# A two-block network on one core: narrow gate products, mLSTM decay rows, the first norm and the compressed values rewritten

## The chip, the cores and the metric

The kernel runs on one core of a Trainium2 chip, as one launch. The metric is the device time of one execution in microseconds; lower is better. All data are float32 in DRAM; the kernel's products have to agree with a float32 reference.

## The reference

512 latent tokens and 256 context tokens of width 1024 go through two hybrid layers; after these the latent tokens alone go through a second block. Cut to what the change touches:

```python
def hybrid_layer(l, x, xc, sc, scc, ...):                 # l = 0, 1
    h = rms_norm(x, norm_g) * (1 + scale[:, None]) + shift[:, None]     # 512 tokens
    hc = rms_norm(xc, norm_g) * (1 + scale_c) + shift_c                 # 256 tokens
    aq, ak, av, az, bq, bk, bv, bo, bz, bg, cq, ... = split_proj(h @ w_in)
    # branch a: differential attention; branch b: mLSTM in both directions, gates from bg (16 columns)
    # branch c: neighbourhood attention; then the three are merged

def mlstm_chunkwise(q, k, v, log_i, log_f, state, with_out):
    ...
    dmat = jnp.where(causal, b[..., :, None] - b[..., None, :] + li[..., None, :], -jnp.inf)
    m_t = jnp.maximum(b + m[..., None], jnp.max(dmat, axis=-1))
    qk = jnp.einsum('bthd,bshd->bhts', qc, kc) * jnp.exp(dmat - m_t[..., None])
    num = a_inter[..., None] * (q @ C) + jnp.einsum('bhts,bshv->bhtv', qk, vc)
    ...

def second block(x):        # hybrid (LRU and retention), ffn, nsa, ffn
    # nsa: 16 heads of width 64 in 4 groups; each head adds three attentions, weighted by
    # sigmoid gates (48 columns of the projection): over compressed keys and values,
    # over selected blocks, and over a window
```

## The kernel before

Activations lie feature-major: eight chunks of 128 features by 768 (or 512) tokens. TensorE takes float32 products in two ways. The large projections split both operands into a high and a low part of a faster format (`slot` casts the raw weights on ScalarE into `whi` and subtracts on VectorE into `wlo`; `make_h` gives `hh` and `hl`) and add three products, hi by hi, hi by lo and lo by hi. `proj` issues these three per chunk, all at line 345; a token-major projection does so at line 402 (`tm_step`). Small products take float32 operands as they are, which shows as two matmul instructions each.

A list scheduler orders each engine's instructions by a simulation of the program; only in `start`, the beginning of layer 0, is the order of PE, DVE and ACT the program's own. Raw weights come through the SP queue into a ring of three tiles, the parts stand in rings of four. PSUM tiles are named `pj` (large) and `s` (small).

The order of the work in one hybrid layer: norm and modulation (`start` in layer 0, `residual_0` in layer 1), branch a, a merge, the gates of branch b (`gates`), its four heads (`mlstm` in each), a merge, branch c, a merge. What the change touches:

- **`start`** (lines 611 to 680) loads the latent chunks `xs`, then the context chunks. ScalarE squares each chunk and VectorE adds it into `ssq` (`sumsq`, line 539), once over the latents and then over the context. Four matmuls with a vector of ones (line 547) sum over the features, `rstd` raises to -1/2 on POOL (line 549), `rows` spreads the result over 128 partitions in PSUM (line 554), `R` is its SBUF copy. Products of a modulation vector (line 486) are turned through line 488 and line 746 into `mod` and the gain `G` (lines 494, 504, 508). A chunk is multiplied by `R` (lines 650, 657, 661, and for chunks 2 to 7 line 673, alternately on VectorE and POOL); then `make_h` makes `hh` on ScalarE (line 576: scale and shift), the same on VectorE in float32 (line 577), and `hl` (line 579). `silu_c`, the input of the modulation, comes first on ScalarE (line 463). Layer 1's `residual_0` multiplies by the row factors at line 1329 and calls the same `make_h`.
- **`gates`**: `proj` makes 16 rows of 768 tokens (24 matmuls of 512 columns and 24 of 256), then six transposes at line 990 turn them. **`nsa_gates`** does the same for 48 rows of 512 tokens (24 matmuls at line 345, four transposes at line 1819). The list scheduler places the latter beside `compress`, whose chain from the compressed keys ends in `kc` and the scores at line 1893.
- **`mlstm`**: for each chunk of 128 tokens and each direction, one transpose of a broadcast column of `Q` (line 1099) writes a matrix whose rows are all equal; VectorE adds the causal mask `MK` and puts the sum into `D` (line 1101), ScalarE takes the exponential, VectorE multiplies by the scores (line 1132), and TensorE takes it as an operand (line 1138). Each direction's `D` has one buffer, so that the next head's first write to it waits for the last use at line 1138. `Q` is ready once per layer (line 1054).
- **`nsa_values`**: per unit (one block of 128 queries of a pair of heads, 32 units), one product of the compressed values, with 64 of the 128 rows (line 1968, two instructions), and then products of the values with the turned weights at line 1972, 64 columns of the array each. It is a generator: `nsa_step` turns four blocks of the next unit's weights (line 746) and lets the generator take one step, by turns.

Of the kernel before, what the change touches and what calls it, by code (L numbers as in the profile page):

```python
# [13 lines left out]
P = 128  # L14
# [148 lines left out]
def make_plan():  # L163
# [5 lines left out]
    pl.tab("arope", 2 * SEQ, da_rope)  # L169

# [108 lines left out]
class Ker:  # L279
# [76 lines left out]

    def pj(self, cols=512, rows=P):
        return self.t(self.psum, [P, 512], F32, "pj", 2)[:rows, :cols]
# [59 lines left out]
    def run(self):  # L418
        tc, nc = self.tc, self.nc
        self.NRING = 4  # L420
        with self.pool("const", 1, "left") as cp, self.pool("ring", 2, "left") as ring, \
# [18 lines left out]
            self.contrib = dram.tile([2, KD, P, TT], F32, name="contrib")  # L440
            self.xsave = dram.tile([KD, P, SEQ], F32, name="xsave")
            self.mods = {}
            self.silu_c()
# [11 lines left out]
    def silu_c(self):  # L455
        nc = self.nc
        self.cl = self.t(self.cp, [P, KD, 32], F32, "cl")
        nc.vector.memset(self.cl, 0.0)
        with self.pool("sc", 1) as sp:
            c = self.t(sp, [P, KD, 2], F32, "c")  # L460
            th = self.t(sp, [P, KD, 2], F32, "th")
            nc.scalar.dma_start(c, self.ap["cv"].rearrange("p (k t) -> p k t", t=2))
            nc.scalar.activation(th, c, AF.Tanh, scale=0.5)
            nc.vector.tensor_scalar_mul(c, c, 0.5)
            nc.vector.scalar_tensor_tensor(self.cl[:, :, 0:2], th, 1.0, c, ALU.add, ALU.mult)

# [74 lines left out]
    def rstd(self, r, ssqs, n):  # L541

        nc = self.nc
        ps = self.s1()
        for i, ssq in enumerate(ssqs):
            for c in range(n):
                nc.tensor.matmul(ps[:, c:c + 1], ssq[:, P * c:P * c + P], self.ones[:, 0:1], start=i == 0, stop=i == len(ssqs) - 1)
# [15 lines left out]
    def make_h(self, l, xs, js, part=None):  # L563
# [4 lines left out]
        for j in js:  # L568
# [42 lines left out]
    def start(self):  # L611

        nc = self.nc
        with self.pool("x0", 8) as xp, self.pool("nt", 1) as sp:
# [9 lines left out]
            ssq = self.t(sp, [P, TT], F32, "ssq")  # L624
# [12 lines left out]
            def stats(c):  # L637
                n = (c.stop - c.start) // P
                r = self.t(sp, [P, 8], F32, "rstd", 2)[:, :n]
                self.rstd(r, [ssq[:, c]], n)  # L640
                return r

            E = mybir.EngineType
            with self.tc.manual_schedule(engines={E.PE, E.DVE, E.Activation}):
                squares(lat)
                rl = stats(lat)
                squares(ctx)
                fin = self.mod_products(units[0], self.s1)
                rows(lat, rl)
                nc.vector.tensor_mul(xs[0][:, lat], rs[:, lat], xs[0][:, lat])  # L650
                fin()
                rc = stats(ctx)
                self.make_h(0, xs, (0,), (lat,))
# [3 lines left out]
                nc.vector.tensor_mul(xs[1][:, lat], R[:, lat], xs[1][:, lat])  # L657
                fin()
                self.make_h(0, xs, (1,), (lat,))
                for j in range(2):  # L660
                    nc.vector.tensor_mul(xs[j][:, ctx], R[:, ctx], xs[j][:, ctx])
                    self.make_h(0, xs, (j,), (ctx,))
                ps = self.tm_banks(NTC, True)
                for s in range(4):
                    j = 2 * s + 2
                    parts = self.tm_step("av", 0, s, ps, 4 * (s == 0), slot)
                    if s < 3:
# [4 lines left out]
                        for i in range(2):  # L672
                            (nc.vector, nc.gpsimd)[i].tensor_mul(xs[j + i], R, xs[j + i])
# [3 lines left out]
                        self.make_h(0, xs, (j,))  # L677
                        next(parts)
                        fin()
                        self.make_h(0, xs, (j + 1,))  # L680
# [243 lines left out]
    def branch_b(self, l):  # L924
        tc, nc, T = self.tc, self.nc, self.T
        full = l == 0
        with self.pool("bb1", 1) as cp:
            with self.pool("bg", 1) as gp:
                G = self.gates(l, cp, gp)
            with self.pool("bb", 2) as sp:  # L930
# [8 lines left out]
                for h in range(4):  # L939
# [23 lines left out]
                    self.mlstm(T // P, h, qk["q"], qk["k"], V, G, hb, ss, sp)  # L963
# [11 lines left out]
    def gates(self, l, cp, sp):  # L975
# [5 lines left out]
        slot = self.slot(("bg", l))  # L981
# [1015 lines left out]
```

## Time and profile before

| | us |
|---|---|
| median of three runs | 3148.14 (3148.11 to 3149.46) |
| the profiled execution | 3147.98 |
| its span, first to last instruction | 3146.2 |
| PE (matmul) busy | 3078.2 |
| VectorE busy | 1797.7 |
| ScalarE busy | 1257.6 |
| POOL busy | 300.9 |

The profile is of one execution. Matmul ends overlap, so the time that one costs is read from start to next start, not from its own duration. In rows of the timeline the columns are start, duration, engine, line, operation, output and inputs, shapes, count, and in brackets the idle time ahead of it and what ended that.

### The profile page before, as it was taken

Reading aid. Unit: us, or ns where it says so; the run is one execution under the profiler, and the core shown is the slowest. Engines: PE = TensorE matmul, PEld = TensorE weight load, DVE = VectorE, ACT = ScalarE, POOL = GpSimd, SP = SyncE. Lnnn points to the kernel's source line nnn. Section 1 sums busy time; section 2 is a strip of 40 time slices with the busy share of each in tenths; the row PEclk is TensorE's granted clock in tenths of the full one; section 3 lists DMA queues with packets and bytes.
Section 4 is the critical chain, followed back from the end, with each engine's and each line's share of the span. In section 5 each row is a group of like instructions: output and inputs, shape, how many; then the busy total and the mean of one; then the engine's idle time right before and its main releaser. Section 6 shows DMA issues by size and latency. Waiting matters only on the chain.

```text
span 3146.2 us, 43890 instructions
## 1 busy us (share of the span) xinstructions
PE 3078.2 (98%) x17322; PEld 2572.0 (82%) x17322; DVE 1797.7 (57%) x3477; ACT 1257.6 (40%) x2382; POOL 300.9 (10%) x284
## 2 busy tenths in 40 slices
PE   7999999999999999999999999999999999999998
PEld 5888788888888888788888877788888788788887
DVE  6776256735574577346455477754433688644433
ACT  4553244325432356234344444332322267632221
POOL 1000000000015000000000400101100022101100
PEclk9999999999999999999999999999999999999999
DMA  6113211332235211311332533233223310022322
GB/s 225 41 34 135 71 60 48 127 115 72 84 138 205 87 49 48 111 54 61 110 104 88 161 100 102 67 101 101 94 94 104 99 41 28 28 94 94 101 92 69
DMA packets 86894, 285.96 MB, mean 91 GB/s; under 512 B 10400, under 2 KB 15264, under 8 KB 86304
## 3 DMA queue, kind: packets, MB, share of 16 engines
q1 hardware_dynamic: 68832, 237.60, 22.6%
q0 software_dynamic: 7424, 28.32, 2.5%
q10 hardware_dynamic: 10432, 17.24, 1.8%
q8 instruction: 136, 2.23, 0.3%
q14 instruction: 70, 0.57, 0.1%
HBM read 268.44 MB, written 14.68 MB: 90 GB/s over the span
## 4 chain that ended last, share of the span: by engine, by line
PE 88%; DVE 7%; issue 2%; ACT 2%; POOL 1%; DMA 0%; ACTq 0%; DVEq 0%; POOLq 0%
PE pj L345 57%; PE s L345 10%; PE s L746 4%; PE s L402 3%; PE s L741 2%; PE pj L402 2%; PE s L742 2%; PE s L1263 1%; PE pj L1972 1%; PE s L878 1%; PE s L1119 1%; DVE kl L737 1%; PE s L1145 1%; PE s L1138 1%; DVE kl L736 1%
## 5 line engine op out<-in xcount | busy, mean ns | idle before, releaser
L345 PE MATMUL pj<-hl,whi 128*128 128x512 f32 (+3 forms) x2696 | 939.5, 367 | 0.3 <-DVE hl L332 0.2
L345 PE MATMUL pj<-hh,whi 128*128 128x512 f32 (+3 forms) x2696 | 936.4, 369 | 2.6 <-ACT hh L331 0.8
L345 PE MATMUL pj<-hh,wlo 128*128 128x512 f32 (+3 forms) x2696 | 938.2, 367 | 0.0
L319 ACT CAST whi<-raw 128x1024 fp32r<-128x1024 f32 (+2 forms) x391 | 405.4, 1038 | 1088.8 <-PE pj L345 841.0
L320 DVE TENSOR_TENSOR wlo<-raw,whi 128x1024 fp32r<-128x1024 f32 (+2 forms) x391 | 488.1, 1249 | 443.4 <-ACT whi L319 434.4
L345 PEld LDWEIGHTS pj<-hh,whi 128*128 128x128 f32 (+2 forms) x2696 | 483.6, 187 | 92.7 <-issue 3.0
L345 PEld LDWEIGHTS pj<-hl,whi 128*128 128x128 f32 (+2 forms) x2696 | 483.0, 187 | 85.0 <-issue 1.9
L345 PEld LDWEIGHTS pj<-hh,wlo 128*128 128x128 f32 (+2 forms) x2696 | 482.9, 187 | 84.3 <-issue 1.7
L345 PE MATMUL pj<-uh,whi 128*128 128x512 f32 (+1 forms) x374 | 141.0, 377 | 0.0
L345 PE MATMUL pj<-ul,whi 128*128 128x512 f32 (+1 forms) x374 | 140.8, 376 | 0.0
L345 PE MATMUL pj<-uh,wlo 128*128 128x512 f32 (+1 forms) x374 | 140.8, 376 | 0.0
L741 PE MATMUL s<-kh,q 128*128 128x256 f32 (+1 forms) x320 | 101.2, 334 | 8.7 <-ACT kh L735 3.3
L700 ACT ACTIVATE th<-pj 128x512 f32<-128x512 f32 x72 | 37.3, 521 | 162.0 <-PE pj L345 150.3
L1715 DVE TENSOR_TENSOR a<-a,pj 128x512 f32<-128x512 f32 x44 | 30.3, 688 | 121.5 <-PE pj L345 121.5
L345 PE MATMUL s<-yh,whi 128*128 128x512 f32 (+1 forms) x288 | 98.7, 357 | 0.0
L345 PE MATMUL s<-yh,wlo 128*128 128x512 f32 (+1 forms) x288 | 98.0, 354 | 0.0
L345 PE MATMUL s<-yl,whi 128*128 128x512 f32 (+1 forms) x288 | 97.8, 354 | 0.0
L1713 POOL TENSOR_TENSOR a<-a,R 128x512 f32<-128x512 f32 x44 | 56.9, 1292 | 409.6 <-DVE a L1712 409.6
L1709 DVE TENSOR_TENSOR a<-pj,R 128x512 f32<-128x512 f32 x44 | 30.4, 691 | 113.5 <-PE pj L345 113.5
L742 PE MATMUL s<-kl,q 128*128 128x256 f32 (+1 forms) x320 | 92.7, 315 | 0.0
L345 PE MATMUL s<-hl,whi 128*128 128x512 f32 (+1 forms) x288 | 89.5, 347 | 0.0
L345 PE MATMUL s<-hh,wlo 128*128 128x512 f32 (+1 forms) x288 | 88.1, 345 | 0.0
(493 smaller groups left out, 4991.4 us busy)
## 6 DMA issues: line engine op xcount, KB each, us to landing
raw<-in_w SPq DMA_DIRECT2D x392, 512.0 KB, 3.4
mraw<-in_w SPq DMA_DIRECT2D x30, 512.0 KB, 4.9
bias<-in_bias ACTq DMA_DIRECT2D x16, 768.0 KB, 4.8
contrib<-cb POOLq DMA_DIRECT2D x16, 384.0 KB, 3.2
ld<-contrib POOLq DMA_DIRECT2D x16, 384.0 KB, 4.0
raw<-in_w SPq DMA_DIRECT2D x16, 384.0 KB, 2.9
contrib<-cb POOLq DMA_DIRECT2D x16, 256.0 KB, 2.6
ld<-contrib POOLq DMA_DIRECT2D x16, 256.0 KB, 3.1
```

What stands on the lines that cost most here:

```text
L319: nc.scalar.copy(hi[:, :width], raw[:, :width])
L320: nc.vector.tensor_sub(lo[:, :width], raw[:, :width], hi[:, :width].bitcast(F32))
L345: self.mm = self.nc.tensor.matmul(ps, wt[:, off + k * mcols:off + (k + 1) * mcols], acts[k][which][:, r], start=first and i == 0, stop=las ...
L402: self.nc.tensor.matmul(ps[c], self.h[k][a][:, P * c:P * c + P], b[:, w], start=k == 0 and pi == 0, stop=k == KD - 1 and pi == 2)
L700: self.nc.scalar.activation(th[:, r], p_, AF.Tanh, scale=0.5)
L736: nc.vector.tensor_sub(kl[a, c], r[a, c], kh[a, c].bitcast(F32))
L737: nc.vector.tensor_sub(kl[b, c], r[a, c], kh[a, c].bitcast(F32))
L741: self.nc.tensor.matmul(out, q[:, qs], kh[:, ks], start=True, stop=False)
L742: self.nc.tensor.matmul(out, q[:, qs], kl[:, ks], start=False, stop=True)
L746: self.nc.tensor.transpose(out[:, P * i:P * i + P], b, self.tab["id"])
L878: nc.tensor.matmul(po, at[:, P * i:P * i + P], V[:, k0 + i, P * h:P * h + P], start=i == 0, stop=i == nb - 1)
L1713: nc.gpsimd.tensor_mul(a, a, self.R)
```

## The change

- **Gates.** A new `narrow` writes the high part of the weights and the low part beside each other into one tile of 2n columns; for each chunk there are two matmuls instead of three, one by `hh` and one by `hl`. The result has 2n rows; the transposes that follow become float32 products by a stacked identity (`sum16`, `sum48`, loaded from the table), which adds the two halves. In `nsa_gates` the row factor is applied after that.
- **Decay rows.** `Q` is transposed once per layer (48 rows), stored into a DRAM tile, and for each head and direction loaded into `D` with every row sent to all 128 partitions. VectorE adds the mask in place.
- **First norm.** In `start` the squares of two chunks are added and then summed by TensorE into one PSUM tile over the four pairs; `silu_c` moves behind the latent squares and the context squares behind the cast of the first weight slot. `make_h` takes the unscaled chunk: one VectorE operation multiplies by `G` and `R`, ScalarE adds the shift only, and `hl` comes from one operation. The separate multiplications by `R` go away, also in layer 1.
- **Compressed values.** `VC` has two forms with zeros in the other half of the rows, so that the product takes all 128 rows. `nsa_values` is no longer a generator: it runs whole ahead of the transposes. A few small tiles move to another ring.

```diff
+    def narrow(self, key, n, outs):
+        raw = self.raw(key)[:, :KD * n].rearrange("p (k f) -> p k f", k=KD)
+        w = self.t(self.ring, [P, SLOT], F32R, "whi", self.NRING)[:, :2 * n * KD].rearrange("p (k f) -> p k f", k=KD)
+        nc.scalar.copy(w[:, :, :n], raw)
+        nc.vector.tensor_sub(w[:, :, n:], raw, w[:, :, :n].bitcast(F32))
+        for ps, r in outs:
+            for k in range(KD):
+                for part in range(2):
+                    nc.tensor.matmul(ps, w[:, k, :], self.h[k][part][:, r], start=k == 0 and part == 0, stop=k == KD - 1 and part == 1)
...
+    def add_squares(self, ps, ssq, n, first, last):
+        for c in range(n):
+            self.nc.tensor.matmul(ps[:, c:c + 1], ssq[:, P * c:P * c + P], self.ones[:, 0:1], start=first and c == 0, stop=last and c == n - 1)
...
-    def make_h(self, l, xs, js, part=None):
+    def make_h(self, l, xs, js, R, part=None):
...
-                nc.scalar.activation(hi[:, r], t[:, r], AF.Identity, bias=sh, scale=sc)
-                nc.vector.tensor_scalar(t[:, r], t[:, r], sc, sh, ALU.mult, ALU.add)
-            c = part[0] if part else slice(0, TT)
-            nc.vector.tensor_sub(lo[:, c], t[:, c], hi[:, c].bitcast(F32))
+                nc.vector.scalar_tensor_tensor(t[:, r], t[:, r], sc, R[:, r], ALU.mult, ALU.mult)
+                nc.scalar.activation(hi[:, r], t[:, r], AF.Identity, bias=sh)
+            for r in part or both:
+                sh = mod[:, j, both.index(r):both.index(r) + 1]
+                nc.vector.scalar_tensor_tensor(lo[:, r], t[:, r], sh, hi[:, r].bitcast(F32), ALU.add, ALU.subtract)
...
             def squares(c):
-                for j in range(KD):
-                    self.sumsq(ssq[:, c], sp, xs[j][:, c], j, c.stop - c.start)
+                n = (c.stop - c.start) // P
+                ps = self.s1()
+                for j in range(0, KD, 2):
+                    sq = [self.t(sp, [P, TT], F32, "sq", 4)[:, c] for _ in range(2)]
+                    for i in range(2):
+                        nc.scalar.activation(sq[i], xs[j + i][:, c], AF.Square)
+                    nc.vector.tensor_add(sq[0], sq[0], sq[1])
+                    self.add_squares(ps, sq[0], n, j == 0, j == KD - 2)
...
-                squares(lat)
-                rl = stats(lat)
-                squares(ctx)
+                rl = squares(lat)
+                silu()
                 fin = self.mod_products(units[0], self.s1)
                 rows(lat, rl)
-                nc.vector.tensor_mul(xs[0][:, lat], rs[:, lat], xs[0][:, lat])
                 fin()
-                rc = stats(ctx)
-                self.make_h(0, xs, (0,), (lat,))
+                self.make_h(0, xs, (0,), rs, (lat,))
                 slot = self.slot(("av", 0, 0))
+                rc = squares(ctx)
                 fin = self.mod_products(units[1], self.s1)
...
-                        for i in range(2):
-                            (nc.vector, nc.gpsimd)[i].tensor_mul(xs[j + i], R, xs[j + i])
...
 # gates
-        slot = self.slot(("bg", l))
-        outs = [(self.pj(SEQ, 16), slice(0, SEQ)), (self.pj(CTX, 16), slice(SEQ, TT))]
-        self.proj(slot, self.h, outs, mcols=16)
+        add = self.load(sp, "sum16")[0:32]
+        outs = [(self.pj(SEQ, 32), slice(0, SEQ)), (self.pj(CTX, 32), slice(SEQ, TT))]
+        self.narrow(("bg", l), 16, outs)
...
-            nc.tensor.transpose(pt[:, 16 * c:16 * c + 16], gs[:, P * c:P * c + P], self.tab["id"][0:16, 0:16])
+            nc.tensor.matmul(pt[:, 16 * c:16 * c + 16], gs[:, P * c:P * c + P], add, start=True, stop=True)
...
+        pq = self.s1()
+        nc.tensor.transpose(pq[0:48, :P], Q.rearrange("p d a h -> p (d a h)"), self.tab["id"])
+        qr = self.t(sp, [48, P], F32, "qr")
+        nc.vector.tensor_copy(qr, pq[0:48, :P])
+        nc.sync.dma_start(self.qrows[l], qr)
...
 # mlstm
+        rows = qrows.rearrange("(d a h) t -> h d a t", d=2, a=6)
+        for d in range(2):
+            nc.sync.dma_start(D[d][:, :n, :], rows[h, d, :n].partition_broadcast(P))
...
-                pe = self.s1()
-                for i, c in enumerate(cs):
-                    nc.tensor.transpose(ch(pe, i), Q[:, d, c, h:h + 1].to_broadcast([P, P]), self.tab["id"])
                 m = len(cs)
-                nc.vector.tensor_add(parts[-1][d], three(pe, m), MK[:, d, None, :].to_broadcast([P, m, P]))
+                nc.vector.tensor_add(parts[-1][d], parts[-1][d], MK[:, d, None, :].to_broadcast([P, m, P]))
...
 # nsa_gates: narrow(("ng", 3), 48, ...), then
-            nc.tensor.transpose(pt[:, 48 * c:48 * c + 48], g[:, P * c:P * c + P], self.tab["id"][0:48, 0:48])
+            nc.tensor.matmul(pt[:, 48 * c:48 * c + 48], g[:, P * c:P * c + P], add, start=True, stop=True)
...
-        VC = self.t(cp, [P, 4, P], F32, "VC")
+        VC = self.t(cp, [P, 2, 4, P], F32, "VC")
         nc.gpsimd.memset(VC, 0.0)
...
 # nsa_step
-        values = self.nsa_values(*ready) if ready else iter(())
+        if ready:
+            self.nsa_values(*ready)
...
-            next(values, None)
-        for _ in values:
-            pass
...
 # nsa_values
-        nc.tensor.matmul(po, VC[rows, g, :], cT[rows, qs], start=True, stop=False)
+        nc.tensor.matmul(po, VC[:, x, g, :], cT[:, qs], start=True, stop=False)
```

## Rows read from the trace of the kernel before

**Rows 1.** The page: busy time, share of the span, instructions of each engine.

```profile
PE 3078.2 (98%) x17322; PEld 2572.0 (82%) x17322; DVE 1797.7 (57%) x3477; ACT 1257.6 (40%) x2382; POOL 300.9 (10%) x284
```

**Rows 2.** Busy time by stretch; last: clock granted, DMA share, GB/s.

```profile
32.00:38.00 6.00, 3.96 (x38) 2.87 (x39) 4.47 (x10) 2.53 (x5) 0.00 (x0) 0.50 0.19 58
...
405.00:595.00 190.00, 189.88 (x1219) 170.31 (x1219) 118.63 (x318) 88.22 (x224) 5.31 (x4) 1.00 0.14 48
...
2523.00:2725.00 202.00, 198.34 (x1522) 158.51 (x1520) 163.44 (x570) 142.70 (x403) 48.65 (x40) 1.00 0.08 25
```

**Rows 3.** Waits of PE, whole span: total us, times, longest.

```profile
PE s L746 <- ACT row L488: 8.2, 3, 7.0
...
PE pj L402 <- DVE hl L579: 1.7, 3, 1.0
...
PE pj L402 <- ACT hh L576: 1.5, 1, 1.5
```

**Rows 4.** Timeline of PE, 361 to 363 us: the gates of layer 0.

```profile
361.61 0.40 PE L345 MATMUL pj<-hh,wlo 128*16 128x512 f32 x1
361.85 0.28 PE L345 MATMUL pj<-hl,whi 128*16 128x256 f32 x1
...
362.85 0.41 PE L990 MATMUL s<-tab_id,gs 16*128 16x16 f32 x4
```

**Rows 5.** Timeline of PE, 2496 to 2499 us: end of compress.

```profile
2496.70 1.94 PE L1893 MATMUL s<-kc,q 128*128 128x64 f32 x16 [0.23 <-DVE kc L1875]
```

**Rows 6.** The tile Q: its writer, first and last start (layers 0, 1).

```profile
L1054 DVE TENSOR_TENSOR Q<-bt,mt x2: 209/209/209, 384.3 to 1351.2; 128x48 f32<-128x48 f32 x2
```

**Rows 7.** Timeline of PE, 430 to 433 us: first decay rows of layer 0.

```profile
430.87 1.47 PE L1099 MATMUL s<-tab_id,Q 128*128 128x128 f32 x12
432.18 0.82 PE L746 MATMUL s<-tab_id,ack 128*128 128x128 f32 x6
```

**Rows 8.** Timeline of PE, 1403 to 1405 us: last use of D, first head of layer 1.

```profile
1403.83 0.61 PE L1138 MATMUL s<-V,D 128*128 128x132 f32 x4
1404.28 0.39 PE L1145 MATMUL s<-C,acq 128*128 128x132 f32 x2
```

**Rows 9.** Timeline of DVE, 1426 to 1428 us: next head's first write of D.

```profile
1426.79 1.29 DVE L1101 TENSOR_TENSOR D<-s,MK 128x512 f32<-128x512 f32 x2 [1.04 <-PE s L1099]
```

**Rows 10.** DMA queue of small loads, whole span: packets, MB, share of 16 engines.

```profile
q10 hardware_dynamic: 10432, 17.24, 1.8%
```

**Rows 11.** Timeline of DVE, 22 to 27 us.

```profile
22.93 2.33 DVE L657 TENSOR_TENSOR x<-R,x 128x512 f32<-128x512 f32 x1
...
25.38 1.59 DVE L504 TENSOR_TENSOR mod<-mod,parsb 128x4 f32<-128x4 f32 x1
```

**Rows 12.** Timeline of POOL, 22 to 29 us.

```profile
22.12 6.58 POOL L673 TENSOR_TENSOR x<-R,x 128x768 f32<-128x768 f32 x3 [1.56 <-ACT R L635]
```

**Rows 13.** Timeline of ACT, at 20 us: cast of the first weight slot.

```profile
20.48 1.03 ACT L319 CAST whi<-raw 128x1024 fp32r<-128x1024 f32 x1
```

**Rows 14.** Timeline of PE, at 34 us.

```profile
34.04 0.69 PE L746 MATMUL s<-tab_id,row 128*128 128x128 f32 x2 [6.96 <-ACT row L488]
```

**Rows 15.** Timeline of PE, 2565 to 2573 us: values of some units.

```profile
2565.59 0.66 PE L1972 MATMUL pj<-pT,V 128*64 128x128 f32 x8
2566.18 0.48 PE L1968 MATMUL pj<-pcT,VC 64*128 64x128 f32 x2
2566.59 0.66 PE L746 MATMUL s<-tab_id,pc 128*128 128x128 f32 x4
...
2568.48 1.97 PE L1972 MATMUL pj<-pT,V 128*64 128x128 f32 x32
...
2571.43 0.69 PE L746 MATMUL s<-tab_id,pr 128*128 128x128 f32 x4
2572.05 0.49 PE L1968 MATMUL pj<-pcT,VC 64*128 64x128 f32 x2
```

**Rows 16.** Line 1972 by itself: idle of its weight loads, us, times.

```profile
  issue: 6.8, 40
```

More of the change, by code (lines that the diff above doesn't have):

```diff
@@ L169, in make_plan @@
     pl.tab("arope", 2 * SEQ, da_rope)
+    for n in (16, 48):
+        pl.tab(f"sum{n}", n, lambda n=n: np.tile(np.eye(n), (2, 1)))
     for l in range(2):
@@ L440, in run @@
             self.contrib = dram.tile([2, KD, P, TT], F32, name="contrib")
+            self.qrows = [dram.tile([48, P], F32, name=f"qrows{l}") for l in range(2)]
             self.xsave = dram.tile([KD, P, SEQ], F32, name="xsave")
             self.mods = {}
-            self.silu_c()
             for l in range(2):
@@ L453, in close_left, with silu_c @@
         self.left = []
-    def silu_c(self):
+    def silu_c(self, sp):
         nc = self.nc
@@ L458, in silu_c, with finish @@
         nc.vector.memset(self.cl, 0.0)
[L459 to L462, printed above, removed]
+        c = self.t(sp, [P, KD, 2], F32, "c")
+        th = self.t(sp, [P, KD, 2], F32, "th")
+        nc.scalar.dma_start(c, self.ap["cv"].rearrange("p (k t) -> p k t", t=2))
+        def finish():
             nc.scalar.activation(th, c, AF.Tanh, scale=0.5)
@@ L541, in rstd, with rstd_of @@
     def rstd(self, r, ssqs, n):
-        nc = self.nc
         ps = self.s1()
         for i, ssq in enumerate(ssqs):
-            for c in range(n):
-                nc.tensor.matmul(ps[:, c:c + 1], ssq[:, P * c:P * c + P], self.ones[:, 0:1], start=i == 0, stop=i == len(ssqs) - 1)
+            self.add_squares(ps, ssq, n, i == 0, i == len(ssqs) - 1)
+        self.rstd_of(r, ps, n)
+    def add_squares(self, ps, ssq, n, first, last):
+        for c in range(n):
+            self.nc.tensor.matmul(ps[:, c:c + 1], ssq[:, P * c:P * c + P], self.ones[:, 0:1], start=first and c == 0, stop=last and c == n - 1)
+    def rstd_of(self, r, ps, n):
+        nc = self.nc
         nc.vector.tensor_scalar(r, ps[:, :n], 1.0 / D, EPS, ALU.mult, ALU.add)
@@ L1811, in nsa_gates @@
         nc = self.nc
-        ps = self.pj(SEQ, 48)
-        self.proj(self.slot(("ng", 3)), self.h, [(ps, slice(0, SEQ))], mcols=48)
-        g = self.t(sp, [P, SEQ], F32, "pT", 6)[:48]
-        nc.vector.tensor_mul(g, ps, self.R[:48])
-        nc.scalar.activation(g, g, AF.Tanh, scale=0.5)
+        add = self.load(cp, "sum48")[0:96]
+        ps = self.pj(SEQ, 96)
+        self.narrow(("ng", 3), 48, [(ps, slice(0, SEQ))])
+        g = self.t(sp, [P, SEQ], F32, "pT", 6)[:96]
+        nc.scalar.copy(g, ps)
         pt = self.s1()
         for c in range(4):
-            nc.tensor.transpose(pt[:, 48 * c:48 * c + 48], g[:, P * c:P * c + P], self.tab["id"][0:48, 0:48])
+            nc.tensor.matmul(pt[:, 48 * c:48 * c + 48], g[:, P * c:P * c + P], add, start=True, stop=True)
         gt = self.t(cp, [P, 4, 16, 3], F32, "gt")
-        nc.vector.tensor_scalar(gt.rearrange("p c h j -> p (c h j)"), pt[:, :192], 0.5, 0.5, ALU.mult, ALU.add)
+        flat = gt.rearrange("p c h j -> p (c h j)")
+        nc.vector.tensor_mul(gt.rearrange("p c h j -> p c (h j)"), pt[:, :192].rearrange("p (c n) -> p c n", c=4), self.rc[:, :, None].to_broadcast([P, 4, 48]))
+        nc.scalar.activation(flat, flat, AF.Tanh, scale=0.5)
+        nc.vector.tensor_scalar(flat, flat, 0.5, 0.5, ALU.mult, ALU.add)
         return gt
@@ L1860, in compress @@
             nc.tensor.matmul(p2[0:64, :124], w2[r, :], gl[r, :], start=True, stop=True)
-            c = self.t(cp, [64, P], F32, "c2", 2)
+            c = small[0:64, P * len(c2):P * len(c2) + P]
             nc.vector.memset(c, 0.0)
@@ L1864, in compress @@
             c2.append(c)
-        tb = self.load(cp, "crope")
+        o, n = self.pl.tabs["crope"]
+        tb = small[:, 3 * P:3 * P + n]
+        nc.scalar.dma_start(tb, self.ap["tab"][:, o:o + n])
         sw = self.t(sp, [P, SEQ], F32, "pcT")[0:64, :P]
@@ L1972, in nsa_values @@
                 nc.tensor.matmul(po[64 * r:64 * r + 64, :], V[:, j, k, g, :], pT[:, P * m:P * m + P], start=False, stop=n == last and m >= len(four) - 2)
-            if n == last:
-                nc.scalar.copy(y[:, qs], po)
-            yield
+        nc.scalar.copy(y[:, qs], po)
 def body(tc, dump=None, **aps):
```

45 lines of the change are left out of this document (21 added, 24 removed).

## Prediction, made before the change was run

> **What bounds the kernel.** I read the page's busy times first: PE works 3078.2 of 3146.2 us [rows 1]. So a microsecond of matmuls removed is a microsecond gained, wherever the other engines keep up, and idle time on them is worth nothing. The table of stretches says where they do: from 405 to 595 us (heads of branch b) PE is busy 189.88 of 190, VectorE 118.63; from 2523 to 2725 us (heads of nsa) PE has 198.34 of 202, but VectorE 163.44 and ScalarE 142.70, which leaves little room there [rows 2]. The third view is PE's waits, in a total idle time of 68 us. Of those that this change could touch, the largest is at the start: 8.2 us for `row`, one of them 7.0. In layer 1's start PE waits 1.5 for `hh` and 1.0 for `hl` [rows 3].
>
> The sum is made against the profiled execution, 3147.98 us (span 3146.2, 1.8 around it), 0.16 below the median of the runs.
>
> **Gates.** A 512-column matmul takes 0.24 us from start to next start [rows 4], and one of 256 columns half of that. I price the new ones, with twice as many weight columns, the same. Per chunk and column range three become two: 8 x (0.24 + 0.12) = 2.9 us less per layer. The six transposes become float32 products of two instructions each. Four transposes last 0.41 [rows 4], about 0.1 each; a float32 product of 132 columns costs 0.225, as two of them lie 0.45 ahead of the next line [rows 8]. Between 0.1 and 0.225 for each, six products add 0 to 0.7 us per layer; I take 0.5, near the full product, because the stationary operand has 128 columns as there. That leaves -2.4 per layer. In nsa 24 matmuls become 16: 8 x 0.24 = -1.9, and four products add 0.4: -1.5. These 24 are also the filler under which `compress` runs: PE waits only 0.23 us before the scores at line 1893 [rows 5]. With eight fewer, a wait of up to 1.9 us could stand there, unless the list scheduler fills in token-major products, of which dozens follow. Sum -6.3, between -4 and -6.8.
>
> **Decay rows.** 80 transposes at line 1099 go away (twelve for each head of layer 0, eight in layer 1: 4 x 12 + 4 x 8). Twelve take 1.31 us from first to the next line [rows 7], 0.109 each: -8.7. One transpose of 48 rows per layer adds about 0.15: -8.4 in all, realised fully, as PE is never idle there [rows 2]. VectorE's additions keep their count and size.
>
> What is new is a chain through DRAM: transpose, copy, store, then on SP two loads a head of 0.39 MB each in layer 0. For the first head `Q` is ready at 384.3 us [rows 6], and line 1099 first reads it at 430.87 [rows 7]: 47 us of cover. For later heads `D` has one buffer, so the load starts after its last use. In layer 1, where a head is shorter, that is 1404.28 [rows 8], and the next write is at 1426.79 [rows 9]: 22 us of cover. No row shows a load of this kind, 1536 packets of 512 bytes a head. The nearest is the queue of small loads: 10432 packets and 17.24 MB in 1.8% of the span of 16 engines [rows 10], 906 us of engine time, which is 87 ns a packet or 53 us a MB. By packets a head's 1536 take 8.4 us on 16 engines, by bytes its 0.79 MB take 2.6. Either fits under the cover, so I take no wait. The loads stand on SP between raw weight loads; one that waits for `D` holds back those behind it, but these run seven ring slots ahead of their use, some 50 us of matmuls. If the cover goes, VectorE waits at line 1101, and behind it stand the head's other VectorE work, the exponentials and line 1138. Bounds -6 to -9.
>
> **First norm.** Here PE waits for one chain. VectorE's line 657 takes 2.33 us, and line 504 takes 1.59 for four columns [rows 11], while POOL runs three multiplications for 6.58 us [rows 12]. PE stands for 6.96 us until 34.04 [rows 14]. From 32 to 38 us its clock is granted at 0.50 (1.2 instead of 2.4 GHz) [rows 2], after that idleness. The change takes POOL's multiplications out. Two VectorE operations of 512 columns take 1.29 elsewhere [rows 9], so line 657 gives back about 1.7, line 504 about 1.4, and the next of its kind as much: 4.5 us of chain. Against it, the context squares now stand behind the cast of the first weight slot, which ran from 20.48 for 1.03 [rows 13]. Eight squares of 256 columns, at some 0.42 (between a quarter and a half of the cast's 1024), then sum, power, rows and copy take some 6 us, to 27.5; one latent and four context operations end near 31, where PE restarts, instead of 34.04. The shorter idleness may also spare part of the half clock, in which PE was busy 3.96 us [rows 2], at most 2 us. I take -4, between -2 (the chain only moves to the squares) and -6.5 (nearly all of the wait). In layer 1's start the multiplication ahead of `hh` and `hl` is merged into one that existed: of the waits of 1.5 and 1.0 I take -2, between 0 and -2.5. Sum -6.
>
> **Compressed values.** Line 1968 uses 64 rows. Its two instructions take 0.41 from start to next start, at 2566.18 [rows 15], although a pair over all rows and 132 columns costs 0.225 [rows 8]. The four transposes ahead of it take 0.62 at 2571.43, against 0.41 at 2566.59 [rows 15]; over the units I read some 0.1 for that. Line 1972 has 640 instructions in 66 unbroken runs. A run of 32 lasts 1.97, 0.06 each, but one of 8 takes 0.59 to the next start [rows 15]: a run's end costs about 0.115. And 40 times its weight load comes late, 6.8 us in all [rows 16], 0.17 each. Before, for 32 units: 32 x (0.41 + 0.1) + 6.8 + 66 x 0.115 = 30.7 us. After, with one run per unit: 32 x (0.225 + 0.17 + 0.115) = 16.3, a gain of 14.4. If the runs stay split at 66, it is 7.2 + 66 x (0.17 + 0.115) = 26.0, a gain of 4.7. VectorE's 163 us, in a stretch then of 188, and ScalarE's copies of the transposes, now in bunches of four, take some of it back: I take -10, between -4 and -14.4. `VC` costs POOL a memset twice as large, off the path.
>
> The Trainium skill speaks against this part: "TensorE: Matmul & The Clock Gate", section "Why this matters for your kernels", says that a single matmul with K = 32 takes the same time as one with K = 128, so that filling the rows would gain nothing. The trace disagrees, 0.41 against 0.225 [rows 8, 15]. By the rule the sum would lose 32 x 0.19 = 6 us.
>
> **Sum.** -6.3 - 8.4 - 6 - 10 = -30.7: 3147.98 - 30.7 = 3117.3, so 3117. All upper ends of the bounds together give 3136, all lower ends 3109.
>
> **Rivals.**
> - The heads of nsa become bound by VectorE and ScalarE, or the list scheduler still splits the runs (then this part doesn't do what it says): it gives -3. For it: VectorE's 163 us [rows 2]; against: PE idles only 3.7 us of 202 there [rows 2]. 3117 + 7 = 3124.
> - A matmul over 64 rows costs no more than one over 128, and the time at line 1968 belongs to a change of shape that stays. For it: line 1972, which has another shape, is near it in every unit; against: the 0.41 at 2566.18, where full-size transposes follow [rows 15]. The gain drops by 6: 3123. This is what the page named above would make of it.
> - The start gains little, because the context squares wait for the weights and their cast [rows 13]: part three gives -2 instead of -6. Against: POOL's stretch [rows 12] is gone anyhow. 3121.
> - Slower: the decay rows land late. If a head's loads take L us after `D` is free, the six later heads lose 6 x (L - 22) at the cover of layer 1. That eats the 30.7 us at L = 27; at L = 35 it is 78, so 3195. For it: every packet of 512 bytes goes to one row, and the loads share SP's queue with 512 KB weight loads; against: 27 is three times my upper bound of 8.4.
>
> **Chances.** Forecast 0.58, heads of nsa bound 0.18, start 0.11, the 64-row rule 0.08, late rows 0.05. The forecast's own range is 3108 to 3127, and the three milder rivals lie inside it; the range of 8 in 10 is 3105 to 3133, which takes in nearly all of the bounds, and on the lower side 4 us for a schedule that happens to fall better. Measurements of this kernel tell about 0.2%, 6.3 us, from no change. Faster than 3141.9: 0.91, nearly all cases but the last; within: 0.05, several parts at their worst or late rows that eat the gain; slower: 0.04, late rows.
>
> **What would show it.** Right: no line 1099, and VectorE's line 1101 without a wait for DMA; PE busy down by some 25 us, to near 3053; 16 matmuls with 32 weight columns per range instead of 24 with 16; PE's wait near 34 us under 4; the pair at line 1968 near 0.22, and some 32 runs of line 1972. Wrong: a wait of VectorE for `D`, a wait of PE over 1 us for the scores of line 1893, or a stretch of the nsa heads shorter by less than 5 us.

## The result, and the profile after

The changed kernel takes 3131.97 us (median of 4 runs, 3127.63 to 3133.06) against 3148.12 before: a ratio of 0.9946, 95% interval 0.9928 to 0.9963. It is 16 us faster, where 30.7 was forecast. The profiled execution took 3131.55 us, its span is 3129.8.

Line numbers have moved: 345 is 347 (369 for the new gate products), 402 is 416, 486 is 502, 746 is 767, 1101 is 1128, 1893 (the scores) is 1925, 1968 is 1997, 1972 is 2001; line 1890 is now the product with the weights `w2`, and in rows of later runs it has the number 1893 or 1861. The tiles in a row say which one is meant. First the page's busy times, which answer to [rows 1].

```profile
PE 3067.3 (98%) x17256; PEld 2580.4 (82%) x17256; DVE 1783.5 (57%) x3472; ACT 1254.6 (40%) x2383; POOL 295.1 (9%) x281
```

PE is busy 10.9 us less, not 25, and 62.5 us idle instead of 68. A busy PE can also be a slow one, so the next view is the table of stretches, in the columns of [rows 2].

```profile
405.00:595.00 190.00, 189.92 (x1198) 169.39 (x1198) 119.92 (x320) 83.64 (x211) 5.92 (x5) 1.00 0.23 69
...
2478.00:2484.00 6.00, 4.36 (x19) 2.78 (x18) 3.22 (x13) 2.02 (x4) 0.00 (x0) 0.81 0.24 87
...
2538.00:2544.00 6.00, 6.00 (x34) 5.07 (x33) 5.11 (x14) 3.45 (x8) 1.56 (x1) 0.65 0.22 78
2544.00:2550.00 6.00, 6.00 (x33) 5.61 (x33) 2.07 (x7) 3.39 (x9) 0.00 (x0) 0.50 0.00 0
```

The heads of branch b are as full as they were. But in nsa the granted clock falls to 0.50, 1.2 instead of 2.4 GHz, where it never fell before. Taking windows of 2 us over the whole span and adding up (1 - granted clock) x 2, the execution before lost 11.0 us of full speed (3.4 at the start, 1.7 near 1988, 5.9 at the very end), the one after 20.2: the new falls are 1.7 near 2483, 5.1 from 2538 to 2550 and 1.7 near 2627, the one at the start is 5.1, and 1.7 near 1974 and 4.9 at the very end are as before. Such a sum is not yet time: where PE has next to nothing left to do, as at the very end, a slow clock costs next to nothing.

PE's waits, in the columns of [rows 3]:

```profile
PE s L566 <- DVE sq L660: 11.2, 3, 5.9
...
PE s L762 <- ACT pT L1989: 1.8, 2, 1.2
...
PE pj L2001 <- ACT pT L1989: 1.6, 3, 0.9
PE s L1890 <- DMA pT<-in_w: 1.6, 1, 1.6
...
PE pj L347 <- ACT y L2002: 1.5, 1, 1.5
...
PE pj L416 <- DVE mod L520: 1.2, 1, 1.2
```

The wait of 7.0 us for `row` is gone, and another stands in its place: the squares (5.9 of the 11.2 are the very first wait, which was 12.7 before; 4.96 are new). In nsa there are four new ones: a DMA at line 1890, and ScalarE's copies in the heads.

The timeline of PE at the gates of layer 0, against [rows 4]:

```profile
354.84 0.39 PE L369 MATMUL pj<-hl,whi 128*32 128x512 f32 x1
355.06 0.40 PE L369 MATMUL pj<-hh,whi 128*32 128x512 f32 x1
...
358.73 1.51 PE L1011 MATMUL s<-sum,gs 32*128 32x16 f32 x12
360.16 0.50 PE L416 MATMUL pj<-whi,hl 128*128 128x512 f32 x1
```

A matmul still takes 0.23, and there are 16 in place of 24, as forecast. The six products that add the halves take 1.43 us, 0.24 each; six transposes took some 0.57.

The tile `D` (operation and count, shortest, median and longest ns, first and last start), against [rows 9]:

```profile
L1128 DVE TENSOR_TENSOR D<-D,MK x24: 414/689/694, 387.6 to 1462.2; 128x512 f32<-128x512 f32 x16, 128x256 f32<-128x256 f32 x8
...
L1122 SPq DMA_DIRECT2D D<-qrows x16: 377/377/537, 382.5 to 1457.4; - x16
...
DMA to landing us min/median/max: 3.2/5.4/7.2
```

The loads land within 7.2 us, and a head's two together took at most 7.9 from the first issue to the second landing, far under the cover of 22 [rows 8, 9]. The first addition starts at 387.6 us now, where line 1099 first ran at 430.87 [rows 7]. Rows that land late, the slower rival, did not come. VectorE does wait for the loads:

```profile
DVE D L1128 <- DMA D<-qrows: 27.7, 11, 6.5
```

The prediction has a wait of VectorE for `D` among the signs of being wrong. It is harmless here: nothing on PE waits for `D`.

The start, timeline of PE, against [rows 14]:

```profile
22.32 3.82 PE L566 MATMUL s<-ones,sq 128*128 128x1 f32 x16 [4.96 <-DVE sq L660]
26.07 1.93 PE L502 MATMUL s<-raw,cl 128*32 128x128 f32 x32
...
34.89 0.44 PE L767 MATMUL s<-tab_id,row 128*128 128x128 f32 x2 [0.85 <-ACT row L504]
35.26 1.08 PE L502 MATMUL s<-raw,cl 128*32 128x128 f32 x32
```

PE stands for the context squares until 22.3, sums them for 3.8 us, and only then comes the second modulation product. The turn that ended the wait at 34.04 before stands at 34.89 now. PE did less of its first projection by then, but stood less, and the clock is full from 32 us on.

The end of compress, against [rows 5]:

```profile
2478.16 0.40 PE L369 MATMUL pj<-hl,whi 128*96 128x512 f32 x1
2480.20 0.43 PE L1890 MATMUL s<-pT,pT 64*64 64x124 f32 x4 [1.65 <-DMA pT<-in_w]
...
2482.76 0.63 PE L416 MATMUL pj<-whi,hh 128*128 128x512 f32 x1
2483.19 0.63 PE L416 MATMUL pj<-wlo,hh 128*128 128x512 f32 x1
```

The DMA is the load of `w2`, the weights that follow the gelu. Its tile is now part of `small`, on the ring `pT`, allocated behind the gelu's; the load is issued at 2475.82 and lands 4.1 us later. In the kernel before it was issued at 2438.3, 54 us ahead of its use. PE waits 1.65 us and then, from 2481.7 on, runs at half clock: 0.43 from start to next start instead of 0.23.

The values of a unit, against [rows 15]:

```profile
2560.13 0.39 PE L1997 MATMUL pj<-pcT,VC 128*128 128x128 f32 x2
2560.44 0.66 PE L2001 MATMUL pj<-pT,V 128*64 128x128 f32 x8
2561.03 0.66 PE L767 MATMUL s<-tab_id,pr 128*128 128x128 f32 x4
```

The pair over all rows takes 0.31 to line 2001, where the one over 64 rows took 0.41. The values stand in 41 unbroken runs instead of 66.

### The profile page after: what moved, and what is told of

The parts are those of the page before. It is cut to its first block, busy times and chain, and to the rows that moved or that the text cites. A ratio compares the mean times of both kernels' runs of the same rounds, so it can differ in the third digit from the quotient of the medians.

```text
span 3129.8 us, 43774 instructions
## 1 busy us (share of the span) xinstructions
PE 3067.3 (98%) x17256; PEld 2580.4 (82%) x17256; DVE 1783.5 (57%) x3472; ACT 1254.6 (40%) x2383; POOL 295.1 (9%) x281
## 4 chain that ended last, share of the span: by engine, by line
PE 87%; DVE 7%; issue 2%; ACT 2%; POOL 1%; DMA 0%; SPq 0%; ACTq 0%; DVEq 0%; POOLq 0%
PE pj L347 57%; PE s L347 10%; PE s L416 3%; PE s L767 3%; PE s L762 2%; PE pj L416 2%; PE s L763 2%; PE s L1290 1%; PE pj L2001 1%; PE s L899 1%; PE s L1146 1%; DVE kl L758 1%; PE s L1172 1%; PE s L1165 1%; DVE wlo L322 1%
## 5 line engine op out<-in xcount | busy, mean ns | idle before, releaser
L347 PE MATMUL pj<-hl,whi 128*128 128x512 f32 (+1 forms) x2656 | 928.2, 368 | 0.3 <-DVE hl L334 0.2
L347 PE MATMUL pj<-hh,whi 128*128 128x512 f32 (+1 forms) x2656 | 923.2, 369 | 4.1 <-ACT y L2002 1.5
L347 PE MATMUL pj<-hh,wlo 128*128 128x512 f32 (+1 forms) x2656 | 925.6, 368 | 0.0
L321 ACT CAST whi<-raw 128x1024 fp32r<-128x1024 f32 (+1 forms) x388 | 404.1, 1042 | 1068.9 <-PE pj L347 850.1
L322 DVE TENSOR_TENSOR wlo<-raw,whi 128x1024 fp32r<-128x1024 f32 (+1 forms) x388 | 487.7, 1257 | 442.1 <-ACT whi L321 432.6
L347 PEld LDWEIGHTS pj<-hh,whi 128*128 128x128 f32 x2656 | 479.3, 188 | 90.2 <-issue 2.7
L347 PEld LDWEIGHTS pj<-hl,whi 128*128 128x128 f32 x2656 | 479.3, 188 | 81.5 <-issue 1.4
L347 PEld LDWEIGHTS pj<-hh,wlo 128*128 128x128 f32 x2656 | 479.3, 188 | 81.2 <-issue 1.7
```

The costliest lines, as they stand in the source:

```text
L321: nc.scalar.copy(hi[:, :width], raw[:, :width])
L322: nc.vector.tensor_sub(lo[:, :width], raw[:, :width], hi[:, :width].bitcast(F32))
L347: self.mm = self.nc.tensor.matmul(ps, wt[:, off + k * mcols:off + (k + 1) * mcols], acts[k][which][:, r], start=first and i == 0, stop=las ...
```

## The experiments

All were timed in five rounds. The kernel before had medians of 3147.77 to 3148.66 us beside them. "By matching steps" means below that the starts of the same matmul are compared in two profiled executions, each from its span's start; the heads of nsa are taken from 2505 us of the kernel before on.

**Each part alone, on the kernel before.** The edit is the part's hunks of the diff above and no other.

e1_gates. 

> The kernel before with the gates part alone. By the terms of the prediction 6.3 us faster (2.4 in each layer, 1.5 in nsa): 3142. Rival, that the products which add the halves cost more than priced (twelve instructions took 1.43 us in the changed kernel, where six transposes took 0.6) and that the 24 matmuls of nsa were cover for the compress chain: 2.0 in each layer and 0 to 1.5 in nsa, 4.0 to 5.5 in all: 3143 to 3144.

Measured: 3144.24 us (3142.63 to 3145.88) against 3147.77, 3.5 faster; ratio 0.9989, 0.9980 to 0.9997. The profiled execution reaches layer 0's line 1030 1.7 us earlier than before, but layer 1's branch a at the old time. PE's timeline at layer 1's start:

```profile
1070.33 1.95 PE L500 MATMUL pj<-raw,cl 128*32 128x128 f32 x32
1072.22 1.54 PE L568 MATMUL s<-tab_id,rstd 128*128 128x128 f32 x6
```

The same two steps take 1.06 and 0.87 in the kernel before and in the whole change: the clock has fallen (0.57 in 1070 to 1074), and the gain of layer 0 is spent. Ahead of it PE waited only 0.34 us but ran matmuls of one column. The same wait and the same matmuls stand there in the kernel before and in the whole change without a fall, so they are not all that it takes. By matching steps the part is worth 1.9 in layer 0, 1.6 in layer 1 and 1.5 in nsa, 5.0; less 1.6 for this fall that is 3.4.

e2_decay. 

> The kernel before with the decay rows alone. By the prediction 8.4 us faster: 3140. Rival, from the trace of the changed kernel, where PE waits 0.6 us for the PSUM bank or the values at the new transpose of Q in each layer: 7.2 us faster, 3141. A late landing of the rows would show as slower; the loads landed within 7.2 us of their issue in the changed kernel, so this is not expected.

Measured: 3141.61 us (3140.44 to 3143.25), 6.2 faster; ratio 0.9980, 0.9971 to 0.9989. VectorE waits 25.8 us for the loads in all, but its additions run so far ahead that PE never waits for them; PE waits 0.61 us in each layer at the transpose of `Q` (its releaser by the profile is ScalarE's `EM`). By matching steps the heads of branch b gain 4.5 in layer 0 and 3.4 in layer 1, 8.0 in all where 8.7 was forecast, and the transpose of `Q` costs 0.8 in each layer instead of 0.15. That makes 6.4, the gain of this execution.

e3_norm. 

> The kernel before with the first norm alone. By the prediction 6 us faster (4 at the start, 2 in layer 1): 3142. Rival, that the context sums, 16 instructions behind the cast, and the second modulation product behind them on PE hold the start: 2.6 us at the start and 1.3 in layer 1, 3.9 in all: 3144.

Measured: 3144.27 us (3143.35 to 3146.54), 3.5 faster; ratio 0.9989, 0.9980 to 0.9998. The rival's size. In the profiled execution, 3145.86, the start gained 1.7 and layer 1's start nothing, as the clock fell there too (1.7 us).

e4_nsa. 

> The kernel before with the compressed values alone. By the prediction 10 us faster: 3138. Rival, that the weights of the compressed keys, now loaded behind the gelu into a tile of another ring, land late, PE stands for them and its clock falls, and that in the heads PE waits for ScalarE's copies: 0 to 3 us faster, 3145 to 3148, with the granted clock under 1 in 2466 to 2560 us.

Measured: 3142.64 us (3141.59 to 3144.16), 5.1 faster; ratio 0.9984, 0.9975 to 0.9993, between the two. PE's timeline shows the late load here too:

```profile
2495.44 0.43 PE L1861 MATMUL s<-pT,pT 64*64 64x124 f32 x4 [1.89 <-DMA pT<-in_w]
...
2496.54 0.63 PE L345 MATMUL pj<-hl,whi 128*48 128x512 f32 x1
```

By matching steps the late load costs 2.9 us, and the heads behind it gain 8.0.

The four parts alone add up to 18.3 us, together they give 16.2. So the shortfall against 30.7 is in the parts, and little is lost between them.

**Part four in two.** g1_rows has `VC` over 128 rows and the moved small tiles, but the generator as before; g2_whole has `nsa_values` whole over 64 rows and nothing else:

```diff
 # g1_rows: nsa_step and nsa_values as before, except
-        nc.tensor.matmul(po, VC[rows, g, :], cT[rows, qs], start=True, stop=False)
+        nc.tensor.matmul(po, VC[:, x, g, :], cT[:, qs], start=True, stop=False)
 # g2_whole: compress as before, nsa_step and nsa_values as after, except
+        rows = slice(64 * x, 64 * x + 64)
+        nc.tensor.matmul(po, VC[rows, g, :], cT[rows, qs], start=True, stop=False)
```

> The kernel before with the compressed values over 128 rows alone; the values still go by turns with the transposes, and the small tiles have moved as in the change. By the terms of the prediction with the runs split, 4.7 us faster, less some 3.6 for the late weights (PE waited 1.9 us and then ran 3.4 us at half clock in the run of the part alone): about 1 faster, 3147. By the rule that 64 rows cost as much as 128, 3 to 4 slower: 3151.

Measured: 3148.62 us (3147.64 to 3149.40) against 3148.49: no change. By matching steps the late load costs 2.7 us (1.7 of them the wait), and the heads give 2.8 back, less than half of the 6 that I read from [rows 8, 15]. PE's timeline shows why, first of this run, then of the kernel before at its last pair:

```profile
2722.20 0.39 PE L1971 MATMUL pj<-pcT,VC 128*128 128x128 f32 x2
2722.43 0.38 PE L746 MATMUL s<-tab_id,pr 128*128 128x128 f32 x2
...
2723.33 0.49 PE L1971 MATMUL pj<-pcT,VC 128*128 128x128 f32 x2
2723.74 0.66 PE L1975 MATMUL pj<-pT,V 128*64 128x128 f32 x8
```

```profile
2723.74 0.49 PE L1968 MATMUL pj<-pcT,VC 64*128 64x128 f32 x2
2724.16 0.66 PE L1972 MATMUL pj<-pT,V 128*64 128x128 f32 x8
```

From start to next start, unrounded, a pair over 128 rows takes 0.223 between these transposes, as priced (0.138 in another place), 0.31 to 0.40 where line 1975 (64 columns) stands on one side of it, and 0.418 where it stands on both. A pair over 64 rows took 0.415 beside nearly every neighbour, full-size ones too. So each change of the array's shape is paid with about 0.1 here. A pair over 64 rows has a change on both sides; over 128 rows only those beside line 1975 stay, and 29 of the 32 pairs stand beside it. This is the second rival in part. The Trainium skill ("TensorE: Matmul & The Clock Gate", section "Why this matters for your kernels") has a single matmul with K = 32 (K are the rows) take the same time as one with K = 128. These traces have 64 rows and not 32; where the changes of shape are alike, they agree: 0.418 and 0.415 between two runs of 64 columns. The 0.41 against 0.225 that the prediction held against the page compares pairs with different neighbours.

> The kernel before with the values of a unit run whole alone, still over 64 rows; the small tiles stay where they were. By the terms of the prediction, about the difference between 14.4 and 4.7, some 9 us faster, less a few for ScalarE: 3139 to 3142. Rival, that PE then waits for ScalarE's copies and its clock falls: 0 to 3 us faster, 3145 to 3148.

Measured: 3145.02 us (3142.53 to 3146.13), 3.5 faster; ratio 0.9988, 0.9979 to 0.9997. Of the waits in [rows 3]'s columns those for ScalarE are new (1.5 for `y`, 1.1 and 0.9 for `pT`), and the clock falls twice in the heads, 1.7 each. The rival holds, a little above its range.

**The late load taken away.** f1_early is the whole change with

```diff
+        small = self.t(sp, [P, SEQ], F32, "pT", 6)
+        w2 = small[:, 2 * P:2 * P + 64]
+        nc.scalar.dma_start(w2, self.ap["w"][self.pl.slots[("w2",)][0], :, :64])
+        o, n = self.pl.tabs["crope"]
+        tb = small[:, 3 * P:3 * P + n]
+        nc.scalar.dma_start(tb, self.ap["tab"][:, o:o + n])
         ph, pb = self.s1(), self.s1()
...
-        small = self.t(sp, [P, SEQ], F32, "pT", 6)
-        w2 = small[:, 2 * P:2 * P + 64]
-        nc.scalar.dma_start(w2, self.ap["w"][self.pl.slots[("w2",)][0], :, :64])
...
-        o, n = self.pl.tabs["crope"]
-        tb = small[:, 3 * P:3 * P + n]
-        nc.scalar.dma_start(tb, self.ap["tab"][:, o:o + n])
```

> The whole change, but the weights of the compressed keys and their table are loaded ahead of the compress products instead of behind the gelu. If the late load costs what the trace shows (1.65 us of wait and 1.7 of half clock), 3.4 us faster than the whole change: 3128.5. Rival, that the wait was hidden by work that moved into it, or that a fall of the clock comes later instead: within 1 us of the whole change, 3131 to 3133.

Measured: 3124.95 us (3123.66 to 3125.86) against 3148.49; ratio 0.9926, 0.9914 to 0.9939. It is 7.0 us faster than the whole change, twice what was expected, and none of its runs is as slow as the fastest of the whole change. PE's timeline:

```profile
2478.82 0.40 PE L369 MATMUL pj<-hl,whi 128*96 128x512 f32 x1
2479.14 0.43 PE L1893 MATMUL s<-pT,pT 64*64 64x124 f32 x4
```

(Line 1893 is line 1890 of the whole change.) There is no wait, no fall of the clock behind it, and none from 2538 to 2550 either. By matching steps 2.9 us come from the load, near the expectation, and 4.0 from the missing fall near 2540. That this fall goes with the load is not shown: e4_nsa has the late load and no such fall, h2_nsa_early (below) the early load and the fall. PE's wait ahead of it is the same, too; first the whole change, then f1_early:

```profile
2537.77 0.50 PE L762 MATMUL s<-kwinh,q 128*128 128x512 f32 x1 [1.18 <-ACT pT L1989]
...
2545.67 3.68 PE L767 MATMUL s<-tab_id,pr 128*128 128x128 f32 x16
```

```profile
2536.00 0.50 PE L762 MATMUL s<-kwinh,q 128*128 128x512 f32 x1 [1.16 <-ACT pT L1989]
...
2541.26 1.97 PE L767 MATMUL s<-tab_id,pr 128*128 128x128 f32 x16
```

The fastest run of the whole change, 3127.63 with a mean granted clock of 0.997 instead of the 0.994 of the profiled one, is 2.7 us above f1_early, about the load's own share.

f2_early_turns is the same with the generator and its turns as before (the last two hunks of the diff undone, `VC` over 128 rows kept). 

> As the run before, and the values again by turns with the transposes, as in the kernel before. If the two falls of the clock in the heads (6.8 us of full speed lost in the profiled run of the whole change) come from running the values whole, they go away and the price is the split runs: 0 to 3 us faster than the run with early weights alone, 3126 to 3129. Rival, that running whole gains more than the clock costs: 3 to 6 us slower than it, 3132 to 3135.

Measured: 3130.44 us (3128.56 to 3131.45), 5.5 slower than f1_early. By the difference the rival is right, 3 to 6 us slower: running whole is worth 5.5 us, less than the 9 that were its share of the term. Its trace has no fall in nsa, but PE waits 4.7 us for VectorE's `pr` there. Of all profiled executions, none of the six with the values by turns has a fall in the heads of nsa, and five of the eight that run them whole have one or two (e4_nsa, h1_start and h4_behind have none). So the falls go with running whole, but not always.

h2_nsa_early is the kernel before with part four alone and the early load. 

> The kernel before with the compressed values alone and the weights of the compressed keys loaded early. If the late load is all that kept this part from its forecast, 8.5 to 10 us faster than before: 3138 to 3140. Rival, that PE's new waits for ScalarE take part of the gain: 6 to 7 us faster, 3141 to 3142.

Measured: 3142.68 us, no faster than part four alone, in two groups: six runs from 3140.24 to 3142.68 with mean granted clocks of 0.995 and 0.996, five from 3146.14 to 3148.72 with 0.993 and 0.994. The profiled execution, 3147.11, is of the second and has half clock from 2554 to 2566, 5.1 us of full speed lost, behind a wait of 1.17 us for ScalarE and without any late load ahead. So the early load doesn't keep this fall away. The middle of the first group is 3141.6, the rival's 6 to 7 us.

h3_ng is f1_early with the gates of nsa made as before. 

> The whole change with early weights, but the gates of nsa made as before, by 24 matmuls and four transposes. By the term of the prediction 1.5 us slower than with the narrow form: 3126.5. Rival, that the eight matmuls were cover for the compress chain and their loss turned into a wait: no slower, 3124 to 3125.

Measured: 3133.96 us (3127.92 to 3134.84), 9 slower than f1_early. The profiled execution is the fastest one; by matching steps it loses 3.0 us to f1_early up to 2505, part of it in a fall of 1.7 us near 2487 that f1_early lacks. The sign is that of the prediction's term; the size is not a measure of the eight matmuls. Where the other runs lost is not on record. The 1.5 by matching steps in e1_gates is the better measure, and it is what was forecast.

**The start.** h1_start is f1_early with the context squares ahead:

```diff
                 silu()
+                sums = ctx_squares()      # ScalarE and VectorE, into four kept tiles
                 fin = self.mod_products(units[0], self.s1)
...
                 slot = self.slot(("av", 0, 0))
-                rc = squares(ctx)
+                rc = ctx_sums(sums)       # TensorE's sums and the power
```

> The whole change with early weights for the compressed keys, and the squares of the context done by ScalarE and VectorE straight behind the latent ones, where both stood idle from 10.8 to 15.9 us, with their sums on TensorE behind the first modulation product. If the start was held by the context squares behind the cast (TensorE waited 4.96 us for them, until 22.3), the second modulation product comes 4 to 5 us earlier and the whole is 4 to 5 us faster than the run with early weights: 3120 to 3121. Rival, that the weights' transfers hold the start anyhow: within 1 us of it, 3124 to 3126.

Measured: 3120.75 us (3119.04 to 3126.47) against 3147.99; ratio 0.9916, 0.9903 to 0.9930; 4.2 faster than f1_early. PE's timeline:

```profile
17.48 3.41 PE L566 MATMUL s<-ones,sqc 128*128 128x1 f32 x16
20.82 1.93 PE L502 MATMUL s<-raw,cl 128*32 128x128 f32 x32
...
29.90 0.44 PE L786 MATMUL s<-tab_id,row 128*128 128x128 f32 x2 [1.10 <-ACT row L504]
```

The product at 26.07 in the whole change (26.53 in f1_early) comes at 20.82, and the turn at 34.89 (35.36) at 29.90; the weights were there.

h4_behind is h1_start with the values whole, but behind the first four transposes:

```diff
-        if ready:
+        if ready and not unit:
             self.nsa_values(*ready)
...
             out.append((four, pT))
+            if ready and b0 == 0:
+                self.nsa_values(*ready)
```

> As h1_start, with the values of a unit still whole, but behind the first four transposes of the next unit instead of ahead of all of them. If PE's waits for ScalarE in the heads of nsa (5.7 us: 1.8 before scores, 1.6 before values, 1.5 before a projection, 0.8 before the compressed values) come from the copies of the transposes standing in a bunch behind the values, part of them goes: 2 to 4 us faster than h1_start, 3117 to 3119. Rival, that ScalarE is short of time whatever the order, or that one more run of values per unit is split off: within 1 us, or up to 3 slower, 3120 to 3124.

Measured: 3120.17 us (3119.07 to 3121.78), within 1 us of h1_start. PE's waits in nsa, first of h1_start, then of h4_behind:

```profile
PE s L786 <- DVE pc L1968: 1.9, 3, 0.6
PE s L781 <- ACT pT L2008: 1.8, 2, 1.2
PE pj L2020 <- ACT pT L2008: 1.6, 3, 0.9
PE pj L347 <- ACT y L2021: 1.5, 1, 1.5
```

```profile
PE s L786 <- DVE pr L1853: 5.1, 11, 0.8
```

The waits for ScalarE are gone, and waits for VectorE's weights stand in their place. The order inside the unit decides only who is waited for.

## Why the forecast came out as it did

The time lies in the range, near its upper end, and the direction was right; the gain is half of the forecast. The prediction has 3136 for all upper ends of the bounds together, but they add up to -4 - 6 - 2 - 4 = -16, which is 3132, the time that was measured. Alone the parts gave 3.5, 6.2, 3.5 and 5.1 us, where these upper ends were 4, 6, 2 and 4. The time lies 1 us inside the range: its width held it, not the sum, and a little more loss would have put it outside.

Of the signs, line 1099 is gone and 16 matmuls stand for 24. But PE is busy 10.9 us less instead of 25, the pair takes 0.31 instead of 0.22, and 41 runs of values are left instead of 32. The heads of nsa are 2.8 us shorter by matching steps, under the 5 that were to show the prediction wrong.

- **Gates, -6.3 forecast, -3.5 alone.** The mechanism held: 16 matmuls for 24, at the same price each. The term for the six products was too small, 0.9 a layer instead of 0.5, at a price just above my upper bound (0.24 against 0.225). The rest is a fall of the clock at layer 1's start, which cost 1.6 in the execution with this part alone. `compress` found other matmuls as cover, so the wait that I feared at line 1893 did not come.
- **Decay rows, -8.4 forecast, -6.2 alone.** All covers held. I left out that the transpose of `Q` itself waits: 0.6 us on PE in each layer. And the 80 transposes were worth 8.0 by matching steps, not 8.7.
- **First norm, -6 forecast, -3.5 alone.** Here a step failed: "end near 31, where PE restarts". I counted the squares, the sum, the power and the copies as one chain behind the cast, but not that TensorE's sums (3.8 us) stand in front of the second modulation product, on the engine whose order is written by hand. The step measured 34.89, in place of 34.04 before, so nothing was gained there; the 2.6 us that layer 0's start gained by its branch a come from less idleness and the earlier full clock. With the squares moved ahead, h1_start came to the same turn at 29.90. The rival of the start was the right one in kind, the context squares behind the cast; and the cure shows that transfers were not the reason. Layer 1's start gave 1.6 in the whole change, its waits of 2.4 being 1.2 now.
- **Compressed values, -10 forecast, -5.1 alone.** This is the step that cost most. I priced `VC`'s memset and nothing else of what moved; the load of `w2` moved too, from a tile of its own to one of a ring behind the gelu, where it lands late: 2.9 us with the half clock behind it. The filled rows bring some 2.8 instead of 6: 0.225 is the price between full-size matmuls, and most pairs keep one change of shape, at line 1972. The whole runs bring 3.5 alone and 5.5 with the early load instead of 9, and 41 runs are left where I counted on 32. The heads of nsa gain 7.9 to 8.4 us in the executions without a fall of the clock there (h1_start, e4_nsa, h4_behind), 6.7 and 6.8 with one (h3_ng, f1_early), 2.8 in the whole change. The first rival, part four at -3, was nearest in the number: up to the compress products the profiled execution had gained 14.8, and at the end it had 16.4. Its mechanism is only a part of it: PE's new waits for ScalarE are there, but no rival named the late load or the falls of the clock in nsa.
- **What stays open.** The falls of the clock in nsa come in some executions and not in others. The one near 2540 stands behind a wait of 1.18 us for ScalarE, but e4_nsa, f1_early, h1_start and h3_ng wait 1.16 or 1.17 at the same step without it. Why the 80 transposes gave 0.7 less than priced is not shown.

With the context squares ahead and the load early, h1_start gains 27.2 us of the 30.7. Its start gives 7.6 of them by matching steps, more than the 4 of the forecast.

## What to carry to other kernels

When a tile moves to another ring, follow its load: it can't start before the ring's turn, and a load that was early for nothing becomes a wait at the point where the data are used. On an engine whose order is written out, price what stands behind the moved step, not only the step's own chain. And on a kernel whose PE is 98% busy, look at the granted clock beside the busy time: a new wait of 1.65 us cost 2.9 with the slow matmuls behind it. When a price is read from a pair of matmuls, look at the shapes of its neighbours too.

## What the runs showed of the hardware

The clock fell to half behind waits that I would have called small: 1.65 us ahead of 2480.2, with slow matmuls from 2481.7 on, and 1.18 us ahead of 2537.77, with slow ones from 2540 to 2550. By matching steps the second fall cost 4.0 us. The 1.65, 1.71 and 1.89 us of the late load were followed by a fall in all three executions that have it (the whole change, g1_rows, e4_nsa); waits of 1.2 us for ScalarE, and 0.34 us with one-column matmuls at layer 1's start, only in some. The kernel with the fewest falls, h1_start, has one alone, at the very end, behind its last matmul.

A change of the array's shape, between 128 and 64 rows or columns, costs about 0.1 us for float32 pairs: mostly 0.22, 0.32 and 0.42 with none, one and two of them (g1_rows).

A load that sends rows of 512 bytes to 128 partitions, 0.39 MB in layer 0, lands in 5.4 us in the middle of 16 and 7.2 at most. A head's two loads in layer 0 took 7.1 to 7.9 together, inside the 2.6 to 8.4 that bytes and packets of another queue gave.
